# Hybrid decoder layer on one core: expert copies written one group ahead of the matmuls

## The chip, the cores and the metric

One core of a Trainium2 chip runs the whole kernel. The metric is device microseconds of one execution; the kernel before has a median of 957.76 us over 3 runs (956.58 to 959.43). The engines are TensorE (PE, with its weight load PEld), VectorE (DVE), ScalarE (ACT), GpSimd (POOL) and SyncE (SP), which issues most DMA transfers. Each works through its own instructions in order.

## The reference

One decoder layer for 256 tokens of width 2048, in float32. The part of interest is the mixture of 32 experts in 4 groups: each token goes to the best group and there to the best two of 8 experts, and each expert is a SwiGLU of width 256:

```
g_probs = softmax(t @ w_router_group);  g_w, g_idx = top_k(g_probs, 1)
weights = softmax(top two expert logits in that group) * g_w
for e in range(32):
    hid = silu(t @ w_gate[e]) * (t @ w_up[e])
    out = out + (hid @ w_down[e]) * comb[:, e:e+1]
```

Before it stand an input projection, attention of 8 heads, a gated linear recurrence and an output projection; after it a gate `sigmoid(norm(h) @ w_ple_gate)` times `p @ w_ple_up`.

## The kernel before

Every expert's gate and up weights (4 chunks of 1 MB, q = 0 to 3, each for 512 of the 2048 input channels) are read once. The experts are taken in rounds r: rounds 0 and 1 hold experts 0 to 3, two each with up to 64 tokens; rounds 2 and 3 the four fullest of the others, two each; rounds 4 to 9 four lighter ones each, with up to 32 tokens. A round walks over the 16 blocks of 128 input channels in 8 groups of two blocks, and in each group PE multiplies the selected tokens' channels with the expert weights into one PSUM bank (`stage1`, line 895, matmuls L901).

Rounds 0 and 1 run interleaved, and then rounds 2 and 3: a loop over i = 0 to 15 (line 1043), where i = 0 to 7 is the first stretch and i = 8 to 15 the second. For each i there are these steps, named here by a letter:

- G(i), the gather (line 851): 8 matmuls of split h with a 0/1 selection matrix bring 256 token slots of two channel blocks into a PSUM bank (L859, L860). The selection for i of 8 and more is written by `select(1)` at i = 6 (line 1068).
- E(i), the evacuation (line 864): block j = 0 on ACT (L870), then j = 1 on DVE (L872), from PSUM into the tile xsT[i % 8].
- C(i), the copies (line 884): for each round of the pair, the slots of its two experts, at an offset held in a register, go from xsT into a buffer xs; rounds 0 and 2 on DVE (L892), rounds 1 and 3 on ACT (L890).
- S(i), the matmuls of `stage1` for both rounds of the pair, first the lower round.
- F(i), what else the loop body writes for DVE: `by_rank` (F(0), lines 651 to 665, which gives the ids that the weight fetches need), `by_rank_rest` (F(1), lines 668 to 695), `token_weights` (F(2)), `token_weights_rest` (F(3), lines 708 to 716), the pieces of `by_count` (F(4), F(5), F(6), then later ones), and in F(6) also `select(1)`, lines 839 to 843. From i = 8 on pieces of `finish` stand there, which turn a round's bank into the hidden values.
- the split of h (line 847, `split_for`): for odd i up to 11, two activations hh on ACT (L576) and two subtractions hl on POOL (L577), for gathers three and more groups later.

In this part the order on PE, DVE, ACT and SP is the order in which the code is written (`manual_schedule`, line 1012); POOL's is set by a scheduler. Before, the loop writes for each i: G(i+1) with its split, C(i), E(i+1), the fetches, S(i), F(i).

Weights live in slots of 1 MB that are reused in rotation. The chunks of rounds 0 and 1 are loaded ahead of the loop and fill the slots; a fetch for round 2 or later (`fetch`, line 1021, issue L1029) goes into the next slot, once the matmuls that read it are done. Three of the early chunks, (expert 3, q 0), (2, 1) and (3, 1), lie in tiles of their own, and the memory of these is given to xsT[2], xsT[3] (that of (3, 0)) and xsT[4] to xsT[7] (lines 809 to 827): E(2) has to follow S(1), and E(4) has to follow S(3).

From round 4 on the rounds run one by one (line 1082), the same C and S with fetches of four experts. `scatter_map` (line 776) makes, in ten steps from group 3 of round 5 on, the scatter matrices from a tile `rows`, which shares one buffer (tag `cmp`) with the tile pTs. In round 8 `ple_up` (line 986) multiplies pT with its weights; at n = 0 it issues the transfer of pT on SP.

Of the kernel before, what the change touches and what calls it, by code (L numbers as in the profile page):

```python
# [10 lines left out]
F32 = mybir.dt.float32  # L11
# [9 lines left out]
P = 128  # L21
S = 256
# [40 lines left out]
def hymba_layer_kernel(ctx, tc, x, xT, gains, w_in, w_f, rnn_v, w_gates, qk_g, b_f, w_out,  # L63
                       w_rt, w_gu, pT, w_pu, *rest):
    nc = tc.nc
# [20 lines left out]
    def bank(pool, tag):  # L86
        return pool.tile([P, 512], F32, tag=tag, name=tag)
# [716 lines left out]
    mw = moe.enter_context(tc.tile_pool(name="mw", bufs=2, side="right", reuse_waits="tile"))  # L804
    gath = ExitStack()
    xsp = gath.enter_context(tc.tile_pool(name="xsp", bufs=1, side="right", reuse_waits="tile"))
# [16 lines left out]
    g = 2  # L823
# [4 lines left out]
    srt = gath.enter_context(tc.tile_pool(name="srt", bufs=1, side="right", reuse_waits="tile"))  # L828
# [18 lines left out]
    def split_for(i):  # L847
        if i % 2 == 1 and i < 13:
            split_h((i + 3) // 2 % 4)

    def gather(i):
        half, g = divmod(i, 8)
        ps = bank(p_t, "t") if g % 2 == 0 else bank(p_o, "o")
        cols = slice(half * S, (half + 1) * S)
        for j in range(2):
            c = slice(((2 * g + j) % 4) * P, ((2 * g + j) % 4 + 1) * P)
            for tb in range(2):
                a, b = hsplit[2 * (i // 2) + tb]
                nc.tensor.matmul(ps[:, j * S:(j + 1) * S], a[:, c], sel01[tb][:, cols], start=tb == 0, stop=False)  # L859
                nc.tensor.matmul(ps[:, j * S:(j + 1) * S], b[:, c], sel01[tb][:, cols], start=False, stop=tb == 1)  # L860
        split_for(i)
        return ps

    def evacuate(i, ps):
        half, g = divmod(i, 8)
        cols = slice(half * S, (half + 1) * S)
        for j in range(2):
            gn_ = gain_sb[:, 1, 2 * g + j:2 * g + j + 1]
            if j == 0:
                nc.scalar.activation(xsT[g][:, j, cols], ps[:, j * S:(j + 1) * S], AF.Copy, scale=gn_)  # L870
            else:
                nc.vector.tensor_scalar(xsT[g][:, j, cols], ps[:, j * S:(j + 1) * S], gn_, None, ALU.mult)  # L872
# [10 lines left out]

    def copies(r, g, offs):
        width = STAGE1[r][0]
        xs = xsp.tile([P, 2, P], F32, tag="xs", name="xs", bufs=3)
        for i, o in enumerate(offs):
            to, src = xs[:, :, i * width:(i + 1) * width], xsT[g][:, :, ds(o, width)]
            if engine_of(r) is nc.scalar:
                nc.scalar.activation(to, src, AF.Copy)  # L890
            else:
                nc.vector.tensor_copy(to, src)  # L892
        return xs

    def stage1(r, g, xs, ws, s1):
        width = STAGE1[r][0]
        for j in range(2):
            kt = 2 * g + j
            for i, w in enumerate(ws):
                k = (kt % 4) * 512  # L900
                nc.tensor.matmul(s1[i * width:(i + 1) * width, :], xs[:, j, i * width:(i + 1) * width], w[:, k:k + 512],  # L901
                                 start=kt == 0, stop=kt == KT - 1)
# [29 lines left out]
    def finish(r, masks):  # L932
        width, who = STAGE1[r]
        s1 = banks.pop(r)
        sc = slot_scalars(masks)
        sg = mw.tile([P, 256], F32, tag="sg", name="sg")
        nc.scalar.activation(sg, s1[:, 0:256], AF.Silu, scale=sc[:, 1:2])  # L937
        yield
        hid = mw.tile([P, 256], F32, tag="hid", name="hid")
        nc.vector.scalar_tensor_tensor(hid, s1[:, 256:512], sc[:, 0:1], sg, ALU.mult, ALU.mult)  # L940
        pt = bank(p_t, "t")
        for f in range(2):
            nc.tensor.transpose(pt[:, f * P:(f + 1) * P], hid[:, f * P:(f + 1) * P], ident)
        yield
        for i, u in enumerate(who):
            at = [nc.scalar.value_load(place[0:1, k, u:u + 1], min_val=0, max_val=m)
                  for k, m in enumerate((LIGHT, SLOTS - LIGHT, SLOTS)) if width == CAP or k == 1]
            for f in range(2):
                part = pt[:, f * P + i * width:f * P + (i + 1) * width]
                if width == CAP:  # L950
                    nc.scalar.activation(store[f][:, ds(at[1], LIGHT)], part[:, ds(at[0], LIGHT)], AF.Copy)
                    nc.scalar.activation(store[f][:, ds(at[2], LIGHT)], part[:, LIGHT:], AF.Copy)
                else:
                    nc.scalar.activation(store[f][:, ds(at[0], LIGHT)], part, AF.Copy)
            yield
# [27 lines left out]

    u, held_up = [], [None, None]

    def ple_up(n):
        if n == 0:
            u.extend(ring2.tile([P, 2048], F32, tag="w", name="u") for _ in range(2))
            for _ in range(2):
                slots.remove(ring2)  # L990
            held_up[0] = srt.tile([P, 2 * S], F32, tag="cmp", name="pTs")
            nc.sync.dma_start(held_up[0], pT.rearrange("p a b -> p (a b)"))
        held_up[1] = gates[n // 2]
        if n % 2 == 0:
            slots.append(gate_pools[n // 2])
        ph, pl = [t.rearrange("p (a b) -> p a b", a=2) for t in split_unit(held_up[0])]
        units = [split_unit(held_up[1][:, (2 * (n % 2) + k) * 512:(2 * (n % 2) + k + 1) * 512]) for k in range(2)]
        for tb in range(2):
            ps = bank(p_o, "o")
            cs = slice(tb * P, (tb + 1) * P)  # L1000
            for k in range(2):
                uh, ul = units[k]
                nc.tensor.matmul(ps, ph[:, k, cs], uh, start=k == 0, stop=False)
                nc.tensor.matmul(ps, ph[:, k, cs], ul, start=False, stop=False)
                nc.tensor.matmul(ps, pl[:, k, cs], uh, start=False, stop=k == 1)
            nc.scalar.activation(u[tb][:, n * 512:(n + 1) * 512], ps, AF.Copy)
# [7 lines left out]
    pairs = FIXED // 2  # L1014
    last = len(STAGE1) - 1
    banks, offs, who, ws, todo = {}, {}, {}, {}, deque()
# [21 lines left out]
    for r in range(pairs):  # L1038
        offs[r] = offsets(r)
        banks[r] = s1_bank(r)  # L1040
    ps = gather(0)
    evacuate(0, ps)
    for i in range(16):
        g = i % 8
        first = pairs * (i // 8)
        if i == 8:
            for r in range(pairs, 2 * pairs):
                banks[r] = s1_bank(r)
        nxt = gather(i + 1) if i < 15 else None
        xs = [copies(r, g, offs[r]) for r in range(first, first + pairs)]  # L1050
        if i < 15:
            evacuate(i + 1, nxt)
        for r in range(first, first + pairs):
            if g % 2 == 0:
                ws[r] = fetch(r, g // 2)
            stage1(r, g, xs[r - first], ws[r], banks[r])
        if i == 0:
            by_rank()
        elif i == 1:
            by_rank_rest()  # L1060
        elif i == 2:
            token_weights()
        elif i == 3:
            token_weights_rest()
        elif i < 8:
            next(counts, None)
        if i == 6:
            select(1)
            for r in range(pairs, 2 * pairs):
                offs[r] = offsets(r)  # L1070
            masks = slot_masks(0)
        if i == 7:
            todo.append(finish(0, masks))
        if i == 11:
            todo.append(finish(1, slot_masks(1)))
        if i in (14, 15):
            next(counts, None)
        if i >= 8:
            step()
    offs[2 * pairs] = offsets(2 * pairs)  # L1080
    parts = scatter_map()
    for r in range(2 * pairs, last + 1):
        banks[r] = s1_bank(r)
        if r > 2 * pairs:
            todo.append(finish(r - 1, masks))
        for g in range(8):
            if g % 2 == 0:
                ws[r] = fetch(r, g // 2)
            xs = copies(r, g, offs[r])
            stage1(r, g, xs, ws[r], banks[r])  # L1090
            if r == 2 * pairs and g in (0, 4):
                todo.append(finish(r - 2 + g // 4, slot_masks(r - 2 + g // 4)))
            step()
            if r > 2 * pairs and g >= 3:
                next(parts, None)
            if r == last - 1 and g % 2 == 0:
                ple_up(g // 2)
            if r < last and g == 6:
                offs[r + 1] = offsets(r + 1)
        masks = slot_masks(r)  # L1100
# [87 lines left out]
    for b, (c0, cn) in enumerate(BLOCKS):  # L1188
        o = [bank(p_o, "o") for _ in range(2)]
        for r in range(1, len(ROUNDS)):  # L1190
# [4 lines left out]
            nxt = down(r, b)  # L1195
# [14 lines left out]
    ws = [gate_chunk(end, n) for n in range(4)]  # L1210
# [220 lines left out]
```

## Time and profile before

| | us |
|---|---|
| median of 3 runs | 957.76 |
| profiled execution | 955.87 |
| its span, first to last instruction | 954.1 |
| PE busy | 843.4 (88%) |
| DVE busy | 450.9 (47%) |
| ACT busy | 360.5 (38%) |
| POOL busy | 79.6 (8%) |
| idle of PE before L901, mostly ended by weight DMAs | 75.0 |

The span is cut by the page into 40 slices of 23.85 us. The mixture of experts begins at about 376 us; the loop over i ends at 477 us, rounds 4 to 9 end at 709 us. Shares of the whole span say little here, since the stages have different limits; the windows and the timeline tell them apart.

### The profile page before, as it was taken

The numbers are of one execution on the slowest core, as the hardware profiler recorded it, in microseconds if no ns is written. First come the engines' busy times: TensorE is split into PE (matmuls) and PEld (weight loads), VectorE is DVE, ScalarE is ACT, GpSimd is POOL, SyncE is SP. The second block draws the span as 40 slices with busy tenths as digits, with TensorE's granted clock in tenths as the row PEclk, the third lists the DMA queues.
The fourth block names the chain that finished last, engine by engine and source line by source line (L and its number), as shares of the span: only waits on it lengthen the run. The fifth ranks groups of instructions, "written<-read, shape, count | busy, mean of one in ns | idle before, by whom it ended". The sixth has DMA issues, their size and how long they took to land.

```text
span 954.1 us, 14463 instructions
## 1 busy us (share of the span) xinstructions
PE 843.4 (88%) x4627; PEld 537.0 (56%) x4627; DVE 450.9 (47%) x1110; ACT 360.5 (38%) x814; POOL 79.6 (8%) x127
## 2 busy tenths in 40 slices
PE   8999999999999998779976766678768999999983
PEld 8999877778778776334432211123223455567652
DVE  7578688665665554463321220113201324454557
ACT  6686866565564543123211000013101335242333
POOL 0000010000100003133120110010100000000005
PEclk9999999999999999889999898979999999999987
DMA  9955453535649747257999999999999999999852
GB/s 315 426 188 192 162 179 133 180 129 181 223 190 424 317 145 296 89 200 287 389 426 424 425 427 426 425 413 381 426 419 418 417 419 419 417 366 314 288 169 92
DMA packets 57876, 290.07 MB, mean 304 GB/s; under 512 B 6848, under 2 KB 7744, under 8 KB 32320
## 3 DMA queue, kind: packets, MB, share of 16 engines
q1 hardware_dynamic: 56816, 286.55, 76.5%
q10 hardware_dynamic: 976, 2.52, 0.7%
q8 instruction: 39, 0.64, 0.3%
q14 instruction: 45, 0.37, 0.1%
HBM read 284.85 MB, written 4.19 MB: 303 GB/s over the span
## 4 chain that ended last, share of the span: by engine, by line
PE 55%; DMA 32%; DVE 7%; ACT 2%; issue 2%; SPq 1%; POOL 0%; DVEq 0%; ACTq 0%
DMA wchunk<-w_gu 16%; DMA wchunk<-w_dn 15%; PE s L901 8%; PE acc L221 4%; PE acc L219 4%; PE acc L220 4%; PE acc L206 3%; PE acc L204 3%; PE acc L205 3%; PE y L901 2%; PE t L546 2%; PE t L545 2%; PE acc L451 2%; PE acc L452 2%; PE acc L450 2%
## 5 line engine op out<-in xcount | busy, mean ns | idle before, releaser
L180 DVE TENSOR_TENSOR ul<-wchunk,uh 128x512 fp32r<-128x512 f32 x296 | 199.8, 694 | 108.8 <-ACT uh L179 107.9
L901 PE MATMUL s<-wchunk,xs 128*32 128x512 f32 (+1 forms) x896 | 177.0, 659 | 75.0 <-DMA wchunk<-w_gu 57.9
L179 ACT ACTIVATE uh<-wchunk 128x512 fp32r<-128x512 f32 x296 | 180.2, 627 | 133.3 <-PE acc L221 47.6
L901 PEld LDWEIGHTS s<-wchunk,xs 128*32 128x32 f32 (+1 forms) x896 | 51.0, 123 | 181.9 <-issue 135.6
L971 PE MATMUL y<-wchunk,store 128*32 128x512 f32 (+3 forms) x640 | 84.1, 525 | 2.2 <-DMA wchunk<-w_dn 1.0
L219 PE MATMUL acc<-uh,xh 128*128 128x512 f32 x192 | 77.0, 401 | 0.0
L220 PE MATMUL acc<-ul,xh 128*128 128x512 f32 x192 | 76.8, 400 | 0.0
L221 PE MATMUL acc<-uh,xl 128*128 128x512 f32 x192 | 76.3, 397 | 0.0
L204 PE MATMUL acc<-xh,uh 128*128 128x256 f32 x256 | 72.3, 283 | 1.0 <-ACT uh L179 1.0
L205 PE MATMUL acc<-xl,uh 128*128 128x256 f32 x256 | 71.8, 281 | 0.2 <-DVE xl L125 0.2
L206 PE MATMUL acc<-xh,ul 128*128 128x256 f32 x256 | 71.4, 279 | 0.2 <-DVE ul L180 0.2
L975 ACT ACTIVATE yh<-y 128x512 fp32r<-128x512 f32 (+1 forms) x45 | 23.0, 512 | 127.5 <-PE y L971 127.5
L976 DVE TENSOR_TENSOR yl<-y,yh 128x512 fp32r<-128x512 f32 (+1 forms) x45 | 26.2, 582 | 84.6 <-ACT yh L975 84.5
L892 DVE COPY xs<-xsT 128x64 f32 (+1 forms) x224 | 32.1, 210 | 58.8 <-PE s L901 50.4
L937 ACT ACTIVATE sg<-s,sc 128x256 f32<-128x256 f32 x8 | 3.8, 475 | 132.2 <-DVE sc L921 132.2
L204 PEld LDWEIGHTS acc<-xh,uh 128*128 128x128 f32 x256 | 48.0, 188 | 1.5 <-ACT uh L179 1.2
L205 PEld LDWEIGHTS acc<-xl,uh 128*128 128x128 f32 x256 | 48.1, 188 | 0.6 <-DVE xl L125 0.4
L206 PEld LDWEIGHTS acc<-xh,ul 128*128 128x128 f32 x256 | 48.1, 188 | 0.5 <-DVE ul L180 0.4
L921 DVE COPY sc<-t 128x2 f32<-128x2 f32 x10 | 1.6, 159 | 96.8 <-PE t L919 96.8
L971 PEld LDWEIGHTS y<-wchunk,store 128*32 128x32 f32 (+1 forms) x640 | 21.5, 113 | 45.7 <-issue 28.2
L911 POOL TENSOR_SCALAR q<-iota,d 128x128 f32<-128x128 f32 x40 | 25.5, 654 | 205.7 <-PE t L919 176.4
L219 PEld LDWEIGHTS acc<-uh,xh 128*128 128x128 f32 x192 | 36.1, 188 | 8.7 <-ACT uh L179 0.4
(396 smaller groups left out, 1351.0 us busy)
## 6 DMA issues: line engine op xcount, KB each, us to landing
wchunk<-w_gu SPq DMA_DIRECT2D x128, 1024.0 KB, 13.8
wchunk<-w_dn SPq DMA_DIRECT2D x96, 512.0 KB, 10.8
wchunk<-w_in SPq DMA_DIRECT2D x37, 1024.0 KB, 4.8
wchunk<-w_out SPq DMA_DIRECT2D x16, 1024.0 KB, 6.6
wchunk<-w_pg SPq DMA_DIRECT2D x16, 1024.0 KB, 8.0
wchunk<-w_dn SPq DMA_DIRECT2D x64, 256.0 KB, 4.9
wchunk<-w_in SPq DMA_DIRECT2D x12, 256.0 KB, 6.1
h<-x SPq DMA_DIRECT2D x2, 1024.0 KB, 13.8
```

What stands on the lines that cost most here:

```text
L179: nc.scalar.activation(uh, raw, AF.Copy)
L180: nc.vector.tensor_tensor(ul, raw, uh.bitcast(F32), ALU.subtract)
L204: nc.tensor.matmul(o, uh[:, cs], a, start=first, stop=False)
L205: nc.tensor.matmul(o, uh[:, cs], b, start=False, stop=False)
L206: nc.tensor.matmul(o, ul[:, cs], a, start=False, stop=last)
L219: nc.tensor.matmul(ps[tb], a[:, c], uh, start=kt == 0, stop=False)
L220: nc.tensor.matmul(ps[tb], a[:, c], ul, start=False, stop=False)
L221: nc.tensor.matmul(ps[tb], b[:, c], uh, start=False, stop=kt == KT - 1)
L892: nc.vector.tensor_copy(to, src)
L901: nc.tensor.matmul(s1[i * width:(i + 1) * width, :], xs[:, j, i * width:(i + 1) * width], w[:, k:k + 512], start=kt == 0, stop=kt == KT - 1)
L971: nc.tensor.matmul(y[i * width:(i + 1) * width, :cn], store[f][:, first + i * width:first + (i + 1) * width], w[:, f, :], start=f == 0, st ...
L976: nc.vector.tensor_tensor(yl, y[:, :cn], yh.bitcast(F32), ALU.subtract)
```

## The change

The loop writes E(i+1) ahead of the copies, and the copies C(i+1) right behind it, so that they stand one group ahead of the matmuls that read them. The split of h follows the copies. xs gets four buffers instead of three and sg one instead of two. The transfer of pT is issued in round 7 at group 0 (`ple_in`), not in round 8.

```
     def gather(i):
...
-        split_for(i)
         return ps
...
-        xs = xsp.tile([P, 2, P], F32, tag="xs", name="xs", bufs=3)
+        xs = xsp.tile([P, 2, P], F32, tag="xs", name="xs", bufs=4)
...
-        sg = mw.tile([P, 256], F32, tag="sg", name="sg")
+        sg = mw.tile([P, 256], F32, tag="sg", name="sg", bufs=1)
...
+    def ple_in():
+        held_up[0] = srt.tile([P, 2 * S], F32, tag="cmp", name="pTs")
+        nc.sync.dma_start(held_up[0], pT.rearrange("p a b -> p (a b)"))
+
     def ple_up(n):
...
-            held_up[0] = srt.tile([P, 2 * S], F32, tag="cmp", name="pTs")
-            nc.sync.dma_start(held_up[0], pT.rearrange("p a b -> p (a b)"))
...
-    ps = gather(0)
-    evacuate(0, ps)
+    evacuate(0, gather(0))
+    xs = [copies(r, 0, offs[r]) for r in range(pairs)]
     for i in range(16):
...
-        nxt = gather(i + 1) if i < 15 else None
-        xs = [copies(r, g, offs[r]) for r in range(first, first + pairs)]
+        now = xs
         if i < 15:
-            evacuate(i + 1, nxt)
+            evacuate(i + 1, gather(i + 1))
+            ahead_of = pairs * ((i + 1) // 8)
+            xs = [copies(r, (i + 1) % 8, offs[r]) for r in range(ahead_of, ahead_of + pairs)]
+            split_for(i + 1)
         for r in range(first, first + pairs):
...
-            stage1(r, g, xs[r - first], ws[r], banks[r])
+            stage1(r, g, now[r - first], ws[r], banks[r])
...
+            if r == last - 2 and g == 0:
+                ple_in()
             if r == last - 1 and g % 2 == 0:
                 ple_up(g // 2)
```

PE's and POOL's instructions stand in the same order in both kernels. On DVE, at i = 0 and 1 (xsT_3969 is the tile of group 1, xsT_4021 that of group 2; L872 is E, L892 is C, L651 to L665 are F(0), L668 begins F(1)), the order before is:

```order
L872 TENSOR_SCALAR xsT_3969<-o,gain_sb 128x256
L651 SCALAR_TENSOR_TENSOR skey<-cns,ku 128x32
...
L665 TENSOR_SCALAR ids<-starts 128x32
L892 ISA
L892 COPY xs<-xsT_3969 128x2x64
...
L872 TENSOR_SCALAR xsT_4021<-t,gain_sb 128x256
L668 TENSOR_SCALAR starts<-starts 128x32
```

and in the changed kernel, where the lines from 862 to 985 have a number lower by one (L871 is E, L891 is C):

```order
L871 TENSOR_SCALAR xsT_3969<-o,gain_sb 128x256
L891 ISA
L891 COPY xs<-xsT_3969 128x2x64
...
L651 SCALAR_TENSOR_TENSOR skey<-cns,ku 128x32
...
L665 TENSOR_SCALAR ids<-starts 128x32
L871 TENSOR_SCALAR xsT_4021<-t,gain_sb 128x256
L891 ISA
L891 COPY xs<-xsT_4021 128x2x64
...
L668 TENSOR_SCALAR starts<-starts 128x32
```

The copies of a group have moved from behind F to directly behind their evacuation, in every round of the loop. On ACT, at the same place, the order before is (L870 is E, L576 the split, L890 C):

```order
L870 ACTIVATE xsT_3968<-t,gain_sb 128x256
L576 ACTIVATE hh<-h 128x512 x2
L890 ISA
L890 ACTIVATE xs<-xsT_3968 128x2x64
...
L870 ACTIVATE xsT_3969<-o,gain_sb 128x256
```

and in the changed kernel:

```order
L869 ACTIVATE xsT_3968<-t,gain_sb 128x256
L889 ISA
L889 ACTIVATE xs<-xsT_3968 128x2x64
...
L869 ACTIVATE xsT_3969<-o,gain_sb 128x256
L889 ISA
L889 ACTIVATE xs<-xsT_3969 128x2x64
...
L576 ACTIVATE hh<-h 128x512 x2
```

The split, two activations, has moved behind two sets of copies. On SP, in round 7, the changed kernel has the transfer of pT behind the first four fetches of that round:

```order
L1020 TENSOR_LOAD ids
L1020 ISA x2
L1030 ISA
L1030 DMA wchunk<-w_gu 128x2048
...
L987 DMA pTs<-pT 128x512
L1030 ISA
L1030 DMA wchunk<-w_gu 128x2048
```

Before it stood at the same place of round 8, one round of 16 fetches later.

## Rows read from the trace of the kernel before

**Rows 1.** Windows: us; PE, PEld, DVE, ACT, POOL busy (instructions); PEclk, DMA share, GB/s:

```profile
379.80:439.05 59.25, 45.54 (x193) 23.08 (x193) 31.79 (x121) 12.13 (x38) 13.30 (x16) 0.86 0.42 160
439.05:477.00 37.95, 37.91 (x197) 17.66 (x196) 11.98 (x36) 13.73 (x46) 10.56 (x16) 1.00 0.94 371
477.00:633.00 156.00, 108.28 (x576) 33.81 (x576) 28.49 (x165) 8.76 (x45) 14.74 (x30) 0.91 1.01 425
396.00:405.00 9.00, 8.78 (x32) 4.07 (x34) 1.44 (x10) 1.55 (x8) 0.00 (x0) 0.74 0.00 0
```

**Rows 2.** Timeline of PE: start, us, engine, line, instruction, [idle before, its releaser]:

```profile
379.82 3.74 PE L901 MATMUL s<-wchunk,xs 128*64 128x512 f32 x16 [0.44 <-PE o L860]
...
396.22 5.94 PE L901 MATMUL s<-wchunk,xs 128*64 128x512 f32 x16 [5.75 <-DVE xs L892]
...
411.84 6.65 PE L901 MATMUL s<-wchunk,xs 128*64 128x512 f32 x16 [3.81 <-DVE xs L892]
...
431.45 0.58 PE L859 MATMUL t<-sel,hh 128*128 128x256 f32 x1 [2.98 <-DVE sel L843]
...
433.81 4.15 PE L901 MATMUL s<-wchunk,xs 128*64 128x512 f32 x16
...
439.05 3.65 PE L901 MATMUL y<-wchunk,xs 128*64 128x512 f32 x16
...
449.56 3.65 PE L901 MATMUL y<-wchunk,xs 128*64 128x512 f32 x16
...
454.29 3.65 PE L901 MATMUL y<-wchunk,xs 128*64 128x512 f32 x16
```

**Rows 3.** Timeline of DVE: E(2), three instructions of F(1), C(2):

```profile
389.88 0.48 DVE L872 TENSOR_SCALAR xsT<-t,gain_sb 128x256 f32<-128x256 f32 x1 [4.25 <-ACT xsT L870]
...
390.98 1.23 DVE L675 CAST starts<-tri 128x32 int32<-128x32 f32 x1
...
392.34 1.13 DVE L677 TENSOR_SCALAR tri<-rnnv 128x32 f32<-128x32 f32 x1
...
395.49 0.17 DVE L693 CAST place<-tri 128x32 int32<-128x32 f32 x1
...
395.94 0.36 DVE L892 COPY xs<-xsT 128x128 f32 x2
```

**Rows 4.** Windows as in rows 1, from first to last of F(1), F(3), F(4), F(5), F(6):

```profile
390.28:395.94 5.66, 0.19 (x2) 0.00 (x0) 5.28 (x22) 1.84 (x5) 2.52 (x2) 0.82 0.77 287
407.83:411.57 3.74, 0.20 (x2) 0.00 (x0) 3.60 (x16) 1.85 (x5) 2.48 (x2) 0.92 0.99 418
412.23:414.49 2.26, 2.26 (x7) 0.80 (x6) 2.23 (x4) 0.00 (x0) 0.00 (x0) 0.50 0.00 0
420.59:424.42 3.83, 3.78 (x22) 1.61 (x18) 3.32 (x20) 0.31 (x1) 0.26 (x1) 1.00 0.48 148
426.45:432.17 5.72, 2.74 (x12) 1.31 (x8) 5.51 (x11) 0.51 (x2) 3.52 (x5) 0.94 1.02 425
```

**Rows 5.** Timeline of ACT, E(2) and E(4):

```profile
389.37 0.48 ACT L870 ACTIVATE xsT<-t,gain_sb 128x256 f32<-128x256 f32 x1 [6.97 <-PE s L901]
...
406.92 0.47 ACT L870 ACTIVATE xsT<-t,gain_sb 128x256 f32<-128x256 f32 x1 [6.29 <-PE s L901]
```

**Rows 6.** Timeline of POOL, the split at i = 2:

```profile
390.92 2.52 POOL L577 TENSOR_TENSOR hl<-h,hh 128x512 fp32r<-128x512 f32 x2 [8.58 <-ACT hh L576]
```

**Rows 7.** Timeline of SP's queue: fourth fetch of round 7; the transfer of pT in round 8:

```profile
579.13 0.33 SPq L1029 DMA_DIRECT2D wchunk<-w_gu  x1
...
618.02 0.37 SPq L992 DMA_DIRECT2D pTs<-pT  x1
```

**Rows 8.** Timeline of DVE, the last reader of `rows`:

```profile
577.86 0.48 DVE L794 SCALAR_TENSOR_TENSOR scat<-rows,slot_id,scat 128x256 fp32r<-128x256 f32 x1
```

**Rows 9.** Timeline of ACT in round 8, the split of pT:

```profile
636.89 0.62 ACT L179 ACTIVATE uh<-pTs 128x512 fp32r<-128x512 f32 x1
```

**Rows 10.** DMA issues of the page: KB each, median us to landing:

```profile
wchunk<-w_gu SPq DMA_DIRECT2D x128, 1024.0 KB, 13.8
```

## The prediction

> **What bounds the kernel now.** I read three things in turn: the busy time of the engines by stage, the order in time on TensorE (PE) inside the slow stage, and for each gap there the engine that ended it. The reader should see in the windows that from 477 us on the DMA engines move 425 GB/s without a break (share 1.01), so the light rounds cost what their bytes cost, while in the first stretch (groups 0 to 7) they stand at a share of 0.42, and between 396 and 405 us at 0 GB/s [rows 1]. They stand because a weight fetch needs a slot, and a slot comes free only when PE has finished the matmuls that read it. So the whole later part of the kernel hangs on when PE leaves the first stretch, not on the DMA itself.
>
> With G(i), E(i), C(i), S(i), F(i) as named in the kernel's section: PE starts S(0) at 379.82 and S(8) at 439.05, 59.2 us for eight groups [rows 2]. Undisturbed, one group takes 454.29 - 449.56 = 4.73 us (S about 3.74, the gather about 1.0), so eight need 37.8. The excess is 21.4 us, all of it in the first stretch; in the second, PE is busy 37.91 of 37.95 us [rows 1, 2]. The timeline shows where the excess sits: S(2) starts after 5.75 us of idling and S(4) after 3.81, both ended by the copies xs on VectorE (DVE), G(8) after 2.98, ended by the selection masks. S(2) and S(4) then take 5.94 and 6.65 us instead of 3.74, with a mean granted clock of 0.74 from 396 to 405 us: part of it ran at 1.2 GHz, after PE had stood still.
>
> Why the copies were late: before S(2), DVE does E(2) at 389.88, then F(1) for 5.66 us, then C(2) at 395.94, and PE starts 0.28 us later [rows 2 to 4]. The copies need nothing of F(1); they only stand behind it on an in-order engine.
>
> **The change part by part.** *Copies ahead of F.* No instruction is added or removed on PE, DVE or ScalarE (ACT); 16 sets of copies and 6 splits move. PE's own order stays. C(i+1) now follows E(i+1) directly, so F(i) runs beside S(i), and what can be late next is the other end: E(i+2) behind F(i). I follow the first stretch with the durations of the rows: E 0.48 on ACT and then 0.48 on DVE, C 0.36, some 0.05 per handover [rows 3, 5].
>
> S(1): C(1) now stands ahead of F(0) and is written two lengths of E and C after G(1), long before PE asks for it, so S(1) starts a pitch after S(0), at 384.55. S(2): E(2) cannot start earlier than the end of S(1), in the order before as in the new one: ACT's E(2) waited 6.97 us for PE, and E(4) 6.29 us [rows 5], because xsT[2] and xsT[4] onward lie in the memory of the early weight tiles. From the end of S(1) at 388.3, E and C take 0.48 + 0.48 + 0.36 + handovers = 1.5 us against 1.0 for G(3), so 0.5 stays: S(2) at 389.8. F(0) is done before that, so E(2) has DVE free. S(3): F(1) without its Pool collisions (below) takes 3.7, until 393.5; E(3) and C(3) follow in 0.9 us; S(3) is due at 394.5 and does not wait. S(4): again 0.5 for the memory of xsT[4]: 399.75. From there DVE works without a break:
>
> C(4) done 399.75; F(3) 3.74, of which about 1.7 was collision: 2.05, until 401.8; E(5), C(5) 0.9, until 402.7; F(4) 2.26, until 405.0; E(6), C(6) 0.9 + 0.4 of collision, until 406.3; F(5) 3.83, until 410.1; E(7), C(7) 0.9, until 411.0; F(6) 5.72, of which 2.0 was collision and 1.7 will be again: 5.4, until 416.4 [rows 3, 4].
>
> PE meanwhile reaches S(5) at 404.5 and S(6) at 409.2 without waiting (C(5) and C(6) are there), and is then ready for G(8) at 413.0. G(8) needs the masks that F(6) writes at its end, so here the wait that is late next appears: G(8) ends some 0.9 us behind the last mask, and S(7) starts at 417.3, 3.4 us late. It started at 433.81: 16.5 us earlier. I leave it the loss of clock that it had (4.15 instead of 3.74 us), so S(8) starts at 422.5 instead of 439.05, again 16.5. That is the 21.4 of excess less 0.5 + 0.5 + 3.4 + 0.5 that stay.
>
> *Collisions with GpSimd (POOL).* Moving the splits behind the copies moves their two POOL subtractions hl, 2.52 us a pair. While such an operation ran, the cast at 390.98 took 1.23 us and the tensor_scalar at 392.34 took 1.13, while a cast of the same form beside no POOL work took 0.17: about 1.0 us is lost to each POOL operation [rows 3, 6]. Before, six such fell on F(1), F(3) and F(6). Where they fall now is not in the trace. Bounds for the chain from C(4) to the masks: nothing (none meets DVE work that it stops), or 4 x 1.05 = 4.2 us. I take 2.1, half of it, since the pair of hl(7) comes out at the masks (POOL does it after the slot masks of round 0, which start when F(5) ends), and the pair of hl(5) falls mostly on F(4), a comparison of 1024 columns and a reduction, before the copies C(6). This leaves the gain between 14.4 and 18.6.
>
> The Trainium skill (SBUF — State Buffer, § Who interferes with whom) says that VectorE and GpSimd share a port pair as an exclusive lock, that copies, casts and tensor_scalar can need it, and a tensor_reduce never does. The two rows agree with it on the cast and the tensor_scalar. By that rule F(4)'s reduction goes free and C(6) waits out the second hl operation, 0.9 instead of my 0.4; the gain would be 16.0.
>
> *Fourth copy buffer.* Two sets of copies are written while two are read, so with three buffers the second one of C(i+1) would wait for the first half of S(i); with four no wait is left. *sg with one buffer.* The next use is at least four groups of 4.73 us later, and its reader follows within a group: nothing. *pT a round earlier.* SP, which also issues the weights, now issues it right behind the first four fetches of round 7. Its buffer is last read by the tenth of the scatter-map steps, at group 7 of round 6, which ended at 578.34 (577.86 + 0.48); the fourth of those fetches went out at 579.13 [rows 7, 8]. So SP does not wait, with 0.8 us to spare, and with four buffers DVE runs another group ahead. Nothing is won either: the split of pT started at 636.89 with no idle time of ACT before it, 18.9 us behind its issue at 618.02, so the transfer did not hold it [rows 7, 9]. I bound this at 0 to 1 us lost, and take 0.
>
> *From S(8) on.* In the second stretch PE is the bound, so it moves as a whole. Fetches 8 and onward of the weights follow the ends of S(7), S(9) and so on, and move with them; the earlier eight have 20 us or more to land. The stream that is full from 477 us on starts 16.5 us earlier and is not shorter, and the rest follows it.
>
> **Sum.** The profiled execution took 955.87 us, 1.77 of it outside the span of 954.1. Less 16.5 this gives 939.4. The median of the runs is 1.89 above the profiled one, so I forecast 957.76 - 16.5 = 941.3.
>
> **The rivals.** *DVE holds PE more than I think.* All four POOL operations of the second half stop DVE (2.1 more), and the clock falls at G(8) so that S(7) takes what S(2) and S(4) took, up to 6.65 instead of 4.15 (2.5 more). For it: DVE is without slack from 399.75 to 416.4. Against it: PE still has something to do until 413. Gain 16.5 - 4.6 = 11.9: 945.9.
>
> *The gain is absorbed by the stream of weights.* If the fetches after S(8) were held by the DMA and not by slots, the end would not move: 957.8. Against it stand the windows with 0.42 and 0 GB/s. The doubt is the second stretch, at a share of 0.94, but its fetches wait for S(7) and later.
>
> *SP stuck at pT.* SP issues in order; if the pT issue had to wait for the last read of its buffer, every weight fetch behind it would wait as well. The place is round 7, behind its first fetch. A landing takes a median 13.8 us [rows 10], so that much wait is covered; the kernel would be slower than before only from 13.8 + 16.5 = 30 us on. That would be the case if the last read stood in round 7 and not in round 6: a round is 618.02 - 579.13 = 38.9 us [rows 7], so 38.9 - 13.8 - 16.5 = 8.6 slower, 966.4. The order of DVE speaks against it: five steps in round 5, five in round 6.
>
> *No POOL collision at all, and no fall of the clock:* gain 19, 938.8.
>
> **How the numbers follow.** A measurement of this kernel tells a difference from about 0.3%, 2.9 us. Forecast, with a gain of 14 to 18.6: 0.72 (939.2 to 943.8). DVE holds PE more (gain 3 to 14, its full price 945.9): 0.17. No collision: 0.04. Absorbed: 0.04. SP stuck or another new wait of that size: 0.03. So faster 0.93, the same 0.04, slower 0.03. The range that leaves out no more than 2 in 10 takes in the bounds of the collisions and part of the first rival: 938 to 947.
>
> **What would show it.** In the changed kernel S(2) and S(4) start within 1.6 us after the end of the matmuls before them and take about 3.7 us; the granted clock stays 1.0 from 382 to 413 us; the one long gap of PE in the stretch stands before G(8), ended by DVE's masks at about 416; S(8) starts at about 422.5; the DMA is full from about 460 us; the pT issue follows its neighbours on SP without a gap, near 563. I am wrong if PE waits for copies elsewhere, if the DMA still has its full share only from 477, or if the rounds from 4 on get longer.

## The result, and the profile after

The changed kernel takes 941.38 us (median of 4 runs, 939.51 to 943.25), against 957.17 for the kernel before (4 runs, 954.87 to 959.43): a ratio of 0.9835, interval 0.9804 to 0.9866, or 15.8 us less. The interval leaves a gain between 12.8 and 18.8 us, so the times alone settle its size only roughly. The forecast was 941.3. The profiled execution took 941.37 us with a span of 939.6, so between the two profiles the gain is 14.5 us.

The timeline of TensorE (PE) in the first stretch answers to [rows 2]. Of each start it shows the time, the duration, the work, and in brackets the idle time before it with the engine that ended it (L900 is now S):

```profile
379.40 3.74 PE L900 MATMUL s<-wchunk,xs 128*64 128x512 f32 x16 [0.45 <-PE o L860]
...
384.21 3.65 PE L900 MATMUL s<-wchunk,xs 128*64 128x512 f32 x16
...
389.25 3.78 PE L900 MATMUL s<-wchunk,xs 128*64 128x512 f32 x16 [0.24 <-DVE xs L891]
...
394.11 3.65 PE L900 MATMUL s<-wchunk,xs 128*64 128x512 f32 x16
...
399.11 3.78 PE L900 MATMUL s<-wchunk,xs 128*64 128x512 f32 x16 [0.20 <-DVE xs L891]
...
408.69 3.65 PE L900 MATMUL s<-wchunk,xs 128*64 128x512 f32 x16
415.51 0.45 PE L859 MATMUL t<-sel,hh 128*128 128x256 f32 x1 [3.17 <-DVE sel L843]
...
417.87 4.24 PE L900 MATMUL s<-wchunk,xs 128*64 128x512 f32 x16
...
423.19 3.65 PE L900 MATMUL y<-wchunk,xs 128*64 128x512 f32 x16
```

The idle time ahead of S(2) fell from 5.75 us to 0.24, and that ahead of S(4) from 3.81 to 0.20, and both take 3.78 us now, at full clock. One long gap is left, before G(8), and it is ended by the masks. S(0) to S(8) take 43.8 us instead of 59.2.

On VectorE (DVE) the copies C(2) now stand ahead of F(1) (behind it in [rows 3, 4]). The rows are C(2), the first row of F(1), the cast that took 1.23 us before, the reduction of F(4), E(6), C(6), and the four instructions that write the masks, of which the third is left out:

```profile
388.97 0.36 DVE L891 COPY xs<-xsT 128x128 f32 x2
389.24 0.17 DVE L668 TENSOR_SCALAR starts<-starts 128x32 int32<-128x32 int32 x1
...
389.95 0.18 DVE L675 CAST starts<-tri 128x32 int32<-128x32 f32 x1
...
403.22 1.09 DVE L736 TENSOR_REDUCE skey<-cmp 128x32 f32<-128x896 bf16 x1
404.57 0.48 DVE L871 TENSOR_SCALAR xsT<-t,gain_sb 128x256 f32<-128x256 f32 x1 [0.27 <-ACT xsT L869]
405.09 0.69 DVE L891 COPY xs<-xsT 128x128 f32 x2
...
412.71 1.34 DVE L842 TENSOR_SCALAR sel<-xsT,pos 128x256 fp32r<-128x256 f32 x1
414.09 1.37 DVE L843 SCALAR_TENSOR_TENSOR sel<-xsT,pos,sel 128x256 fp32r<-128x256 f32 x1
...
415.76 0.48 DVE L843 SCALAR_TENSOR_TENSOR sel<-xsT,pos,sel 128x256 fp32r<-128x256 f32 x1
```

GpSimd (POOL) shows where its subtractions hl fall now, the pairs of i = 2, 4 and 6 (the first was at 390.92 in [rows 6]):

```profile
394.52 2.51 POOL L577 TENSOR_TENSOR hl<-h,hh 128x512 fp32r<-128x512 f32 x2 [10.41 <-ACT hh L576]
402.80 2.77 POOL L577 TENSOR_TENSOR hl<-h,hh 128x512 fp32r<-128x512 f32 x2 [5.77 <-ACT hh L576]
...
412.65 2.52 POOL L577 TENSOR_TENSOR hl<-h,hh 128x512 fp32r<-128x512 f32 x2
```

The first pair falls into idle time of DVE, and F(1) ran from 389.24 to 392.90 without meeting one. The second runs until 405.57, over most of F(4), E(6) and the start of C(6). The third lies on the first two mask instructions, which take 1.34 and 1.37 us; the second two, clear of it, take 0.34 and 0.48. One more pair, of i = 0 at 381.60, lies on F(0), where DVE has 2.90 us to spare before E(2).

ScalarE (ACT) still waits for PE before E(2) and E(4), as in [rows 5]:

```profile
387.94 0.47 ACT L869 ACTIVATE xsT<-t,gain_sb 128x256 f32<-128x256 f32 x1 [5.89 <-PE s L900]
...
397.80 0.47 ACT L869 ACTIVATE xsT<-t,gain_sb 128x256 f32<-128x256 f32 x1 [1.90 <-PE s L900]
```

The windows (columns as in [rows 1]: us; busy PE, PEld, DVE, ACT, POOL; granted clock, DMA share, GB/s) show the stretch up to the masks, the fall of the clock at G(8), the second stretch, the full stream of weights, and most of round 8:

```profile
379.00:415.00 36.00, 32.50 (x160) 16.08 (x160) 26.34 (x107) 12.15 (x37) 13.41 (x16) 1.00 0.59 226
...
415.00:420.00 5.00, 4.36 (x16) 2.53 (x18) 2.61 (x11) 0.99 (x3) 0.17 (x1) 0.66 0.49 205
...
423.20:461.00 37.80, 37.55 (x197) 16.72 (x196) 11.95 (x36) 14.07 (x44) 10.54 (x16) 1.00 0.94 373
461.00:617.00 156.00, 108.64 (x576) 34.37 (x576) 27.86 (x165) 8.76 (x45) 14.89 (x30) 0.91 1.01 425
...
625.00:660.00 35.00, 30.80 (x167) 13.19 (x165) 12.16 (x47) 12.70 (x29) 0.53 (x2) 0.97 0.89 368
```

The DMA is full from 461 us instead of 477, at the same 425 GB/s. On SyncE's (SP's) queue the transfer of pT follows its neighbours without a gap (compare [rows 7]); the first row holds the third and fourth fetch of round 7:

```profile
562.85 0.90 SPq L1030 DMA_DIRECT2D wchunk<-w_gu  x2
563.85 0.37 SPq L987 DMA_DIRECT2D pTs<-pT  x1
564.47 0.33 SPq L1030 DMA_DIRECT2D wchunk<-w_gu  x1
```

Not all of the gain reaches the end. S(8) is 15.86 us earlier, and the first long run of S in round 8 is 15.84 earlier (633.43 before, 617.59 after), but the span is 14.5 shorter. In round 8, before:

```profile
633.43 1.88 PE L901 MATMUL s<-wchunk,xs 128*32 128x512 f32 x10 [1.44 <-DMA wchunk<-w_gu]
643.21 1.92 PE L901 MATMUL s<-wchunk,xs 128*32 128x512 f32 x16
```

and after:

```profile
617.59 3.31 PE L900 MATMUL s<-wchunk,xs 128*32 128x512 f32 x10 [1.52 <-DMA wchunk<-w_gu]
...
628.51 1.92 PE L900 MATMUL s<-wchunk,xs 128*32 128x512 f32 x16
```

The same ten records took 3.31 us instead of 1.88 after a similar idle time. The mean granted clock was 0.57 from 617.5 to 621 us, and 1.00 from 633.4 to 635.3 in the kernel before. S of group 1 then follows S of group 0 after 10.92 us instead of 9.78. The matching window of the kernel before had a DMA share of 0.94, that of the changed one 0.89:

```profile
641.00:676.00 35.00, 29.27 (x162) 11.99 (x161) 10.89 (x37) 12.54 (x29) 0.00 (x0) 0.97 0.94 387
```

A share lower by 0.05 over 35 us is about 1.7 us of transfers, near the 1.4 us missing at the end. The change doesn't bring this loss in every run: in five of the eight variants below these ten records took 1.88 us, and in the other three (early masks, split first, odd pieces) 3.28 to 3.51.

### The profile page after: what moved, and what is told of

Read it like the earlier page. It is cut to its first block, busy times and chain, and to the rows that moved or that the text cites. A ratio compares the mean times of both kernels' runs of the same rounds, so it can differ in the third digit from the quotient of the medians.

```text
span 939.6 us, 14433 instructions
## 1 busy us (share of the span) xinstructions
PE 840.2 (89%) x4627; PEld 534.4 (57%) x4627; DVE 448.2 (48%) x1110; ACT 360.9 (38%) x814; POOL 80.0 (9%) x127
## 4 chain that ended last, share of the span: by engine, by line
PE 65%; DMA 23%; DVE 7%; ACT 2%; issue 1%; POOL 0%; SPq 0%; DVEq 0%; ACTq 0%
DMA wchunk<-w_gu 17%; PE s L900 7%; PE y L970 5%; PE acc L221 4%; PE acc L219 4%; DMA wchunk<-w_dn 4%; PE acc L220 4%; PE o L981 3%; PE acc L206 3%; PE acc L205 3%; PE acc L204 3%; PE y L900 2%; PE t L545 2%; PE t L546 2%; PE s L1174 2%; PE acc L451 2%
## 5 line engine op out<-in xcount | busy, mean ns | idle before, releaser
L900 PE MATMUL s<-wchunk,xs 128*32 128x512 f32 (+1 forms) x896 | 176.2, 662 | 62.1 <-DMA wchunk<-w_gu 53.1
L900 PEld LDWEIGHTS s<-wchunk,xs 128*32 128x32 f32 (+1 forms) x896 | 49.0, 121 | 166.8 <-issue 137.5
L891 DVE COPY xs<-xsT 128x64 f32 (+1 forms) x224 | 31.4, 210 | 40.9 <-PE s L900 25.9
```

## The experiments

The theory: the whole gain comes from the copies of the first stretch no longer standing behind F; what is left there is the masks ahead of G(8); and the time at which PE leaves the stretch passes to the end one to one. The rivals: part of the gain belongs to the second stretch, the fourth buffer, the moved split, or the earlier pT; or the stream of weights would absorb a shift. All are variants of the changed kernel. The two stretch-only variants, the early masks and the delay of PE share runs of the kernel before with a median of 957.28 us (20 runs), the other four 957.81 (9 runs).

**Copies ahead in the first stretch only.** Groups 0 to 7 as in the changed kernel, 8 to 15 as before, pT in round 8:

```
+    def early_c(i):
+        return i < 8
...
+        if early_c(i):
+            now = xs
+        else:
+            if i < 15:
+                split_for(i + 1)
+            now = [copies(r, g, offs[r]) for r in range(first, first + pairs)]
...
-            if r == last - 2 and g == 0:
+            if r == last - 1 and g == 0:
```

> Copies ahead of F only for groups 0 to 7; groups 8 to 15 in the order of the kernel before; pT fetched in round 8 as before; four xs buffers and one sg buffer as in the changed kernel. My theory (the whole gain is made in the first stretch, pT and the second stretch are worth nothing): S(8) starts at about 423, the DMA is full from 461, the time is 941.4 us, within 2 us of the changed kernel. Rival (the reordering of the second stretch or the earlier pT carries part of the 15.8 us): at least 3 us longer, 944.5 or more.

Measured: 941.96 us (940.44 to 944.75), ratio 0.9846 [0.9824, 0.9869]. The gain is all there. The timeline of PE has S(7) and S(8):

```profile
417.91 5.82 PE L900 MATMUL s<-wchunk,xs 128*64 128x512 f32 x16
424.79 3.65 PE L900 MATMUL y<-wchunk,xs 128*64 128x512 f32 x16
```

S(7) starts within 0.04 us of the changed kernel's 417.87; S(8) is 1.6 us later because S(7) took 5.82 us. The granted clock was 0.50 from 415.5 to 422.0 us here, and in the changed kernel only from 415.7 to 419.0. The span, 938.7 us, is 0.9 shorter than the changed kernel's all the same: from S(8) to the end this run took 2.5 us less, 1.1 of it in round 8, where group 1 followed group 0 after 9.78 us.

**Copies ahead in the second stretch only.** The same with

```
+    def early_c(i):
+        return i >= 8
```

> The reverse: copies ahead of F only for groups 8 to 15, groups 0 to 7 in the order of the kernel before, pT in round 8. My theory: S(8) starts at 439 as before, and the time is that of before, 957.2 us, within 2 us. Rival (the second stretch carries a part): 954 or less.

Measured: 955.86 us (954.53 to 959.29), ratio 0.9993 [0.9978, 1.0008]: no difference. S(4) again waits 3.81 us for its copies, and S(8) starts 0.9 us later than before (439.05), because S(7) took 5.74 us instead of 4.15:

```profile
411.40 6.44 PE L900 MATMUL s<-wchunk,xs 128*64 128x512 f32 x16 [3.81 <-DVE xs L891]
...
439.99 3.65 PE L900 MATMUL y<-wchunk,xs 128*64 128x512 f32 x16
```

**Three copy buffers**, and two of sg:

```
-        xs = xsp.tile([P, 2, P], F32, tag="xs", name="xs", bufs=4)
+        xs = xsp.tile([P, 2, P], F32, tag="xs", name="xs", bufs=3)
...
-        sg = mw.tile([P, 256], F32, tag="sg", name="sg", bufs=1)
+        sg = mw.tile([P, 256], F32, tag="sg", name="sg")
```

> The changed kernel with three xs buffers and two sg buffers, as before. My theory (the second set of C(i+1), on ACT, then waits for the first half of S(i), which is over long before S(i+1) asks for it): S(8) within 0.5 us of 423.2, the time 941.4, within 2 us. Rival (the fourth buffer is what lets the copies run ahead): PE waits for ACT's copies in each group, 0.5 to 2 us each, 945 or more.

Measured: 942.17 us (941.96 to 942.96), ratio 0.9842 [0.9829, 0.9856], not to be told from the changed kernel.

```profile
405.67 0.51 ACT L889 ACTIVATE xs<-xsT 128x128 f32 x2 [1.43 <-PE s L900]
...
417.57 5.49 PE L900 MATMUL s<-wchunk,xs 128*64 128x512 f32 x16
424.13 3.65 PE L900 MATMUL y<-wchunk,xs 128*64 128x512 f32 x16
```

The first row is ACT's half of C(6): with three buffers it waits 1.43 us for the matmuls that read the buffer, as the expectation said (405.09 in the changed kernel, after a wait for DVE). PE does not feel it. S(7) starts 0.30 us earlier than in the changed kernel, as S(0) does (379.09 against 379.40). The 0.94 us by which S(8) is later comes from the longer S(7), 5.49 us against 4.24. So PE waited no longer than in the changed kernel, and the fourth buffer is worth nothing that shows.

**The masks earlier.** `select(1)` at i = 2 instead of 6, which takes away what G(8) waited for:

```
+        if i == 2:
+            select(1)
         if i == 6:
-            select(1)
```

> The changed kernel with the selection masks for groups 8 to 15 made in F(2) instead of F(6). My theory (the one wait left in the first stretch is PE before G(8), for the end of DVE's chain): the 3.17 us wait goes, so does the half clock behind it (0.9 in G(8), 0.6 in S(7)); S(8) starts about 4.8 us earlier, at 418.4, and the time is 936.6 us. Rival (DVE's chain is the bound of the stretch, so that another wait takes the place of this one): S(8) gains less than 2 us, 939.5 or more. Rival (the stream of weights absorbs it): S(8) moves by 4.8, the time by less than 1.

Measured: 935.46 us (934.64 to 937.3), ratio 0.9771 [0.9749, 0.9792].

```profile
413.55 3.65 PE L900 MATMUL s<-wchunk,xs 128*64 128x512 f32 x16
418.28 3.65 PE L900 MATMUL y<-wchunk,xs 128*64 128x512 f32 x16
```

S(8) follows S(7) after 4.73 us, the undisturbed length of a group, and starts at 418.28, 4.9 us earlier than in the changed kernel. Without the gap the clock doesn't fall either: the mean granted clock is 1.00 from 379 to 418 us. So the masks and the clock behind them were what was left. By the medians 5.9 us reach the end. By the two profiles it is 4.0 (span 935.6): from S(8) to round 8 this run took 1.5 us longer than the changed kernel's.

**PE held up.** 88 extra matmuls (128x128) ahead of S(8), into a bank whose content is overwritten:

```
+            for _ in range(88):
+                nc.tensor.matmul(banks[pairs][:, :P], ident, ones, start=True, stop=True)
```

> The changed kernel with 88 extra 128x128 matmuls on PE between S(7) and G(9), 0.114 us each as the row of 30 of them in the kernel before, 10.0 us in all; their result is overwritten. My theory (everything behind the first stretch moves one to one with its end): 951.4 us. Rival (the stream of weights would run at its own pace, so the end of the first stretch matters little): less than 945.

Measured: 961.75 us (960.92 to 962.41), ratio 1.0042 [1.0027, 1.0058]. The size of the delay was misread: the trace records such an f32 matmul twice, so the duration that I took for one was that of half a matmul. The row of the extra matmuls shows 176 records for 88 in the code:

```profile
423.23 19.92 PE L1051 MATMUL y<-ones,ident 128*128 128x128 f32 x176
444.02 2.37 PE L900 MATMUL y<-wchunk,xs 128*64 128x512 f32 x10
```

The delay was 19.9 us. S(8) starts at 444.02, 20.8 later than in the changed kernel (0.9 of it from a later S(0)), and the span is 960.7, 21.1 longer. The mechanism holds all the same, at twice the size that was meant: what PE loses at S(8) the whole kernel loses, and the stream of weights absorbs none of it.

**The split ahead of the evacuation**, as in the kernel before, with the copies left ahead:

```
-            evacuate(i + 1, gather(i + 1))
+            nxt = gather(i + 1)
+            split_for(i + 1)
+            evacuate(i + 1, nxt)
...
-            split_for(i + 1)
```

> The changed kernel with the split of h ahead of evacuation and copies, where it stood before. My theory: ACT's copies come 1.1 us later in the odd groups, which S does not feel; the POOL pair of group 5 falls on C(5) and the end of F(3) instead of C(6); hl(7) still follows the slot masks and falls on the selection masks. S(8) between 423.0 and 424.2, the time 941.4 to 942.5. Rival (moving the split was needed): 944 or more.

Measured: 944.69 us (944.31 to 946.45), ratio 0.987 [0.9855, 0.9885], about 3 us slower than the changed kernel. My theory missed here and the rival holds: the moved split is a working part of the change. The timeline of PE shows S(3), G(8), S(7) and S(8):

```profile
395.50 3.78 PE L900 MATMUL s<-wchunk,xs 128*64 128x512 f32 x16 [1.11 <-DVE xs L891]
...
417.61 0.58 PE L859 MATMUL t<-sel,hh 128*128 128x256 f32 x1 [3.89 <-DVE sel L843]
...
419.97 5.03 PE L900 MATMUL s<-wchunk,xs 128*64 128x512 f32 x16
...
426.09 1.50 PE L900 MATMUL y<-wchunk,xs 128*64 128x512 f32 x5
```

POOL's pairs now start earlier, at 390.27 and 401.32 instead of 394.52 and 402.80:

```profile
390.27 2.66 POOL L577 TENSOR_TENSOR hl<-h,hh 128x512 fp32r<-128x512 f32 x2 [7.39 <-ACT hh L576]
401.32 2.53 POOL L577 TENSOR_TENSOR hl<-h,hh 128x512 fp32r<-128x512 f32 x2 [8.38 <-ACT hh L576]
```

and so they lie on F(1) and F(3), as they did in the kernel before. On DVE:

```profile
390.46 1.14 DVE L677 TENSOR_SCALAR tri<-rnnv 128x32 f32<-128x32 f32 x1
...
392.16 0.82 DVE L684 TENSOR_TENSOR tri<-tri,iota 128x28 f32<-128x28 f32 x1
...
401.76 0.89 DVE L712 TENSOR_SCALAR gm<-oh,wt 128x32 f32<-128x32 f32 x1
402.69 1.20 DVE L713 SCALAR_TENSOR_TENSOR gm<-oh,wt,gm 128x32 f32<-128x32 f32 x1
```

The same four instructions take 0.18, 0.19, 0.23 and 0.25 us in the changed kernel. Each pair of collisions costs DVE 1.6 us. The first makes C(3) late, so that S(3) waits 1.11 us. The second adds 0.7 us net to the chain that ends in the masks, since C(6) and E(6) no longer lose anything there. The third pair misses the masks (0.35 and 0.48 us each) and holds up two instructions of F(6) just before them, so the expectation was wrong there too. S(8) is 2.9 us later than in the changed kernel: 0.2 from the start of S(0), 1.2 at S(3), 0.7 more at G(8) (417.61 against 415.51, 2.1 in all), and 0.8 in S(7), which took 5.03 us instead of 4.24.

**pT in round 8 again:**

```
-            if r == last - 2 and g == 0:
+            if r == last - 1 and g == 0:
```

> The changed kernel with pT fetched in round 8 as before. My theory: the earlier fetch is worth nothing, 941.4 within 2 us; if anything 0.6 us shorter, since the 0.26 MB then pass in round 8, where the DMA engines stand for 4.0 us in the changed kernel, and no longer in the full stream. Rival (pT was late for its split): 943 or more.

Measured: 941.24 us (938.72 to 943.42), ratio 0.9824 [0.9808, 0.984], the same as the changed kernel. The earlier pT is worth nothing.

**A version that beats both.** The masks early as above, and the pieces of `ple_up` in round 8 at odd groups. Two groups use one set of four fetched chunks, and the four slots come free only after the second; a piece of `ple_up` between the two delays that (in the changed kernel S of group 0 starts at 617.59 and S of group 1 at 628.51):

```
-            if r == last - 1 and g % 2 == 0:
+            if r == last - 1 and g % 2 == 1:
```

> The kernel with the masks in F(2) (935.5 us), and the four pieces of ple_up in round 8 behind groups 1, 3, 5, 7 instead of 0, 2, 4, 6. My theory (part of the gain of the first stretch is lost in round 8, because the first piece stands between the two groups that free four weight slots, and the DMA engines stand for 4.0 us in the changed kernel, 5.7 us with the masks early, 2.5 us before): S(8) stays at 418.3, the standing time in round 8 falls under 1 us, the time is 931.5 us, between 930 and 933. Rival (the loss is the clock's, wherever the pieces stand): 934.5 to 936.5.

Measured: 932.88 us (932.5 to 934.07), ratio 0.9744 [0.973, 0.9757]: 2.6% faster than the kernel before. S of group 1 now starts at 618.32, 4.95 us behind group 0, although the ten records of group 0 again took 3.36 us, so the rival of the clock fails. The window of round 8 has no hole in the stream. With the masks early alone the share was 0.50 from 620 to 625 us and 0.92 from 625 to 660; here it is:

```profile
625.00:660.00 35.00, 29.77 (x170) 12.69 (x162) 13.45 (x55) 12.37 (x30) 2.51 (x4) 1.00 1.01 425
```

Against the early masks alone the times are 2.6 us apart, but the two intervals just overlap, so the size of this second step is less certain than its mechanism.

## Why the prediction was right

- *What bounds the kernel* held. The excess over 4.73 us a group, 21.4 us before, is 43.8 - 37.8 = 6.0 us after, so 15.4 us went in the stretch, where 16.5 were forecast. The stretch-only variants place all of it in groups 0 to 7, and the delayed variant shows that it passes to the end about one to one. That rules out the rival of a gain absorbed by the weights.
- *S(2) and S(4)* were to keep 0.5 us each for the memory of the early weight tiles. They are 5.04 and 5.00 us behind S(1) and S(3), so 0.3 stayed of each, and ACT's E(2) and E(4) are still released by PE.
- *F(1) and F(3) without collisions* was a term of the sum (3.7 and 2.05 us; measured 3.7 and 2.1). It rested on the moved split without my saying so, and my later expectation treated that move as neutral. The variant with the split in its old place shows what it carries, 2.9 us at S(8), 0.8 of that by the clock in S(7).
- *Collisions between C(4) and the masks* were taken as 2.1 us, between bounds of 0 and 4.2. Measured: 0.33 on C(6), and 0.99 and 0.89 on the two mask instructions, 2.2 in all. The sum had 0.4 at C(6) and 1.7 in F(6), and there they fell: the second is the pair of hl(7) (i = 6) on the masks. The reduction of F(4) took 1.09 us under the pair of hl(5) (i = 4), as it did in the variant with the old split where it met no POOL work. The Trainium skill (SBUF — State Buffer, § Who interferes with whom) states that a reduction never contends, and this agrees. The price of 0.9 us that I worked out for C(6) by that rule was too high: C(6) came behind E(6) only at 405.09, when 0.48 us of the pair were left, and lost 0.33.
- *The masks before G(8)* came as forecast: the last ends at 416.24 (forecast 416.4), and the variant with early masks removes the gap. That the time fits so well is a balance of two errors. C(4) was done about 0.6 us earlier than forecast (S(0) started earlier and S(2) and S(4) waited less), and the chain behind it was about 0.5 us longer; it did have a break, the 0.27 us that E(6) waited for ACT.
- *What comes behind the masks* I mis-sized. G(8) was to end 0.9 us after the last mask; S(7) starts 1.63 after it. PE had stood for 3.17 us, the mean granted clock from 415 to 420 us is 0.66, and the gather's matmuls, not only S(7), ran partly at 1.2 GHz. That cost the gather 0.7 us that the sum did not have. S(7) itself lost 0.6 us of clock, where 0.5 was left to it. The rival in which DVE holds PE more had this fall of the clock, but in S(7), at up to 2.5 us. In this profile S(7) was 0.1 over what was left to it; in the variant with copies ahead in the first stretch only it was 1.7 over. So part of that rival was alive, and the changed kernel's profile was lucky. S(8) came at 423.19 and not at 422.5. As S(0) started 0.42 us earlier than before, its gain was 15.86.
- *That the rest of the kernel only follows* failed by a little: of 15.86 us at S(8), 14.5 reached the end of the profiled run. The loss lies in round 8, where the first ten records of group 0 took 3.31 us instead of 1.88 and the fetches behind them came later. The prediction put no term there, though it named longer rounds from 4 on as a sign of being wrong. The sign came true by 1.1 us in this run, by the clock and not in every variant. From S(8) to the end the kernel before took 515.1 us, the changed one 516.4 and the variants without the odd pieces 513.9 to 517.3, so "one to one" holds within about 3 us.
- *That 941.3 met 941.38* is luck. The forecast took a gain of 16.5 us from a median of 957.76; the gain was 15.8, from a median of 957.17. The gain was 0.7 us short and the kernel before 0.6 us faster. The runs of each kernel spread over some 4 us.
- *The fourth buffer, sg and pT* were put at nothing, and are nothing. The buffer's reason was half right: with three, ACT does wait (1.43 us at C(6)), but PE never notices. SP did not wait at pT.

What stays open is how long the clock stays low after the gap. S(7) took 4.24 us in the changed kernel, 4.47 with pT back and 4.54 with PE held up, but 5.03 with the split first, 5.49 with three buffers and 5.82 with copies ahead in the first stretch only. PE stood before G(8) for 3.16 to 3.18 us in each of them but the split-first one (3.89). The stretch at a granted clock of 0.50 is about twice as long in the last three as in the first three (415.5 to 422.0 us in the last, 415.7 to 419.0 in the changed kernel). No run shows what decides between the two. That moves S(8) by up to 1.6 us from one kernel to the next.

## What to carry to other kernels

On an engine that works in order, copy what the bottleneck engine reads next as soon as it can be copied, and put the work that nobody waits for behind it; then look at once for what is late next, here the masks, which brought S(8) forward by another 4.9 us for one moved call. When an instruction that feeds GpSimd is moved, follow where its GpSimd work lands on VectorE, and give it a price by the rows. A buffer that others wait for should be freed before side work is done, not after it.

## What the runs showed of the hardware

- A short VectorE instruction that was held up under a GpSimd subtraction of 128x512 lost 0.3 to 1.1 us: casts, tensor_scalars and copies, but also operations with two inputs in SBUF (0.48 to 1.37 us for the mask, 0.25 to 1.20 for one of F(3)). Not every one under such a pair was held up: L676, a tensor_tensor, took 0.18 us at 392.13 in the kernel before, inside the pair of 390.92, about where the first of its two subtractions ended. The section of the Trainium skill named above states that two SBUF inputs contend with GpSimd's reads; the rows of the mask and of F(3) agree.
- After a similar idle time of about 1.5 us, the same ten matmul records of round 8 took 1.88 us once and 3.31 once, at a mean granted clock of 1.00 and of 0.57 around them. Which of the two it is was not visible in the idle time before them alone.
- The trace records one 128x128 f32 matmul twice (176 records for 88), at 0.226 us for the instruction (19.92 / 88).
